# Up projection of a gated MLP: from TensorE transposes to 32x32 transposes on VectorE and regrouping transfers within SBUF

## The chip, the cores and the metric

The kernel runs on one core of a Trainium2 chip. The metric is the device time of one execution in microseconds, the median of three runs. The work of the core is spread over TensorE (PE), VectorE (DVE), ScalarE (ACT), GpSimd (POOL) and the queue of SyncE (SP), which issues nearly all DMA transfers.

## What is computed

One decoder layer on 256 tokens of width 2048, in float32: a parallel mixer (two kinds of attention), a cross attention into 256 memory tokens, and a gated MLP with a causal convolution of width 3 along the tokens, then a last RMSNorm. The change is in the MLP alone:

```python
def conv_ffn(h, w_up, conv_w, conv_b, w_down):
    u = causal_depthwise_conv(h @ w_up, conv_w, conv_b)
    gate, val = u[..., :D_FF], u[..., D_FF:]
    return (jax.nn.silu(gate) * val) @ w_down
```

`D_FF` is 5632, so `w_up` has 2 x 5632 columns. The convolution mixes each feature's own values of three neighbouring tokens, with three weights and a bias per feature.

## The kernel before, in words

**Products.** Every projection is cut into units of 512 output columns (`product`, line 177). A unit keeps two PSUM tiles, one for each block of 128 tokens, and runs over the rows of the weight in blocks of 128. The weights come in transfers of four such blocks (1 MB, `raw`, three buffers, issued on SP at line 190). Each transfer is split in two halves of two row blocks. For precision each half is split into a high and a low part (`split_w`): ACT casts the high part (line 162), DVE subtracts to get the low part (line 163), into two pools of three buffers. Then twelve matmuls run on a half: two row blocks, two token blocks, three products of parts (lines 168 to 170). A unit of the up projection has 16 row blocks, so four transfers, eight halves and 96 matmuls.

**Work between the products.** `tick` is called once per half, while the program is written. Work that is left for later is a generator in `tasks`; `spawn(gen, d)` puts it in the program d halves later, and each `yield n` leaves n halves more. A scheduler then orders the instructions of PE, ACT, DVE and POOL. The queue of SP is kept in the order in which the program is written.

**The MLP (lines 553 to 589).** There are 22 up units. Unit i holds 256 gate columns and the 256 value columns that go with them. When its matmuls are done, ACT copies both PSUM tiles into SBUF, scaled by the norm of each token (`zu`, line 588). Two halves later `gated` turns the unit feature-major: eight PE transposes of 128 x 128 (line 562) into PSUM tiles `uT`, so that features lie on partitions and tokens run along the free dimension. The convolution then takes, for each of four blocks of 128 features, one ACT instruction (line 568) and two DVE instructions (lines 570 and 572) on 256 tokens. Sigmoid, two products and a split into two parts (`gT`, lines 576 to 580) make the left operand of the down projection (`dn`), which follows with 44 row blocks per unit.

```python
    for i in range(KF // 2):
        ps = product(x2T, w_up, i, KD, f"up{i}")
        z = [wk.tile([P, U], F32, tag="w2", name=f"zu{t}") for t in range(NT)]
        for t in range(NT):
            nc.scalar.activation(out=z[t], in_=ps[t], func=AF.Copy, scale=r2[:, t:t + 1])
        spawn(gated(i, z), 2)
```

**Pools.** `b4` has 34 buffers of 4 KB per partition: in the MLP the eight tiles of `x2T`, the four of the residual `xr`, and the `gT` tiles as they are made, 22 at the end.

Of the kernel before, what the change touches and what calls it, by code (L numbers as in the profile page):

```python
# [16 lines left out]
P = 128  # L17
S = 256          # tokens
NT = S // P      # token blocks
D = 2048  # L20
KD = D // P      # 128-row blocks of the model width
FF = 5632
KF = FF // P
U = 512          # columns of one product unit
KB = 4           # 128-row blocks per weight transfer
# [6 lines left out]
# columns of the packed per-partition parameters  # L32
# [13 lines left out]
def hybrid_layer(ctx: ExitStack, tc: tile.TileContext, x, xT, mem, memT, gmix, par, gfin,  # L46
# [28 lines left out]
    # additive masks of the diagonal blocks: [q, k] -> 0 where k <= q (k < q), else NEG  # L75
# [8 lines left out]
    # Work that is emitted between the products: generators that yield the number of  # L84
    # half blocks of weights to let pass before they go on.
# [27 lines left out]
    def split(dst, src, gains=None):  # L113
        """dst[:, 0] + dst[:, 1] = src, or src * gain, in two parts of 12 bits.
        dst [P, 2, 2, S], src [P, 2, S]; gains: a [P, 1] column per 128-row block."""
# [10 lines left out]

    def transposed(dst, src, n, name, gains=None):
        """dst: act tiles of the 4 row blocks n*4.. of the transpose; src [P, NT, U]."""
# [16 lines left out]
    def rstd(ss, n, width, name):  # L145
        """(sum over the last axis of ss [P, n, m] / width + EPS) ** -0.5 -> [P, n]"""
# [19 lines left out]
    def mm3(out, a, b, start=True, stop=True):  # L166
        """out (+)= (a[0] + a[1]).T @ (b[0] + b[1]) without the product of the two low parts."""
        nc.tensor.matmul(out, lhsT=a[0], rhs=b[0], start=start, stop=False)  # L168
        nc.tensor.matmul(out, lhsT=a[0], rhs=b[1], start=False, stop=False)  # L169
        nc.tensor.matmul(out, lhsT=a[1], rhs=b[0], start=False, stop=stop)  # L170
# [6 lines left out]
    def product(xs, w, u, kt_n, name, pieces=None, before=None, heap=False):  # L177
        """x @ w[:, unit u] for both token blocks -> two PSUM tiles [P, U].
        pieces: 128-row blocks per transfer; before(kt): called ahead of the transfer from kt on."""
# [25 lines left out]
    def load_split(src, gains, i, name):  # L205
        """Split act tile i of a transposed input [P, KD, S] in DRAM, scaled by gains."""
# [27 lines left out]
    def proj_T2(ps, r, name):  # L234
        """Evacuate a unit scaled by r and transpose it: act tiles of heads 0, 1 and 2, 3."""
# [7 lines left out]
    def proj_T(ps, r, name, rotate=False):  # L243
        """Evacuate a unit scaled by r and transpose it: [P (dim), 4 (head), S]."""
# [21 lines left out]
    def proj_n(ps, r, name):  # L266
        """Evacuate a unit scaled by r: [P (token), NT, U]."""
# [5 lines left out]
    def attn_T(a, name):  # L273
        """Causal weights of one head [q block][P, K] -> [P (key), 3 * P]:
        keys 0 for both query blocks, then keys 1 for query block 1."""
# [8 lines left out]
    # differential attention  # L284
    oaT = [None] * 4

    def diff_head(h):
        qT, kT, v, hh = qa[h // 4], ka[h // 4], va[h // 4], h % 4
        # scores of the two maps, in a bank each: query block 0 in 0:P, query block 1 in P:3 * P
# [62 lines left out]
    # stick-breaking attention, two heads at a time  # L352
    obT = [None] * 4

    def stick_pair(g):
        aw = [[], []]
        for i in range(NT):
# [14 lines left out]
            # softplus(z) = max(z, 0) + ln(1 + exp(-|z|)), zero where masked  # L372
# [27 lines left out]
    # the input projection in units; the attention of a group of heads runs between the products  # L400
# [21 lines left out]
    # lam = exp(q1.k1) - exp(q2.k2) + LAM_INIT, negated, on all partitions  # L422
# [33 lines left out]
    # branch projections, gated and merged  # L456
# [18 lines left out]
    # output projection and residual  # L475
# [77 lines left out]
    gT = [None] * (KF // 2)  # L553

    def gated(i, z):
        us = []
        for part in range(2):          # gate, value
# [154 lines left out]
```

## Time and profile before

| | |
|---|---|
| time, median of 3 runs (lowest to highest) | 1521.37 us (1520.65 to 1521.76) |
| span of the profiled execution | 1518.9 us; the median of the runs lies 2.5 us above it, which is taken as the time around the span |
| busy, share of the span | PE 99%, DVE 59%, ACT 52%, POOL 4% |
| granted TensorE clock | full (2.4 GHz) in all 40 slices |
| DMA | 287.78 MB, 189 GB/s over the span |
| up projection, from about 753 to 1250 us | 22 units |

The profile is one execution. "Busy" counts the time in which an engine has an instruction at work. Each view below is one question put to the trace of that execution; times in a timeline count from the start of the span.

### The profile page before, as it was taken

The page shows a single profiled execution, that of the slowest core. Times are in us where ns is not written, and L with a number is a line of the kernel's source. Part 1 is how long each engine was busy: PE and PEld are TensorE (multiplying, and loading weights), DVE is VectorE, ACT ScalarE, POOL GpSimd, SP SyncE. Part 2 cuts the span into 40 slices and gives each one's busy share as a digit, 9 for nine tenths or more (in the row PEclk, how much of TensorE's full clock was granted, in tenths as well). Part 3 has the DMA queues.
Part 4 walks back from the last instruction along what each step waited for, and adds up shares of the span by engine and source line. Part 5 has one row for each costly group of instructions (what it writes and reads, how often), then busy time and mean ns, then how long its engine had stood idle before and what let it go on. Part 6 is the DMA issues. An engine that isn't in the chain of part 4 may idle for free.

```text
span 1518.9 us, 17599 instructions
## 1 busy us (share of the span) xinstructions
PE 1503.4 (99%) x6904; PEld 1243.2 (82%) x6904; DVE 896.7 (59%) x1131; ACT 784.7 (52%) x1074; POOL 53.7 (4%) x72
## 2 busy tenths in 40 slices
PE   8999999999999999999999999999999999999997
PEld 6878788888888888888888888888888888888886
DVE  5575666564444565664666667666666666444562
ACT  6454555465555344664565555555555555344441
POOL 0202000000000010000000000000000000000010
PEclk9999999999999999999999999999999999999999
DMA  9544444445555556755355555555555555655561
GB/s 349 187 159 152 162 166 167 167 166 194 194 194 193 183 193 246 265 197 192 139 191 174 189 194 178 183 194 185 179 191 192 174 190 192 222 194 192 197 230 73
DMA packets 44003, 287.78 MB, mean 189 GB/s; under 512 B 5008, under 2 KB 5008, under 8 KB 11152
## 3 DMA queue, kind: packets, MB, share of 16 engines
q1 hardware_dynamic: 43488, 286.13, 54.5%
q8 instruction: 54, 0.88, 0.2%
q10 hardware_dynamic: 432, 0.53, 0.1%
q14 instruction: 29, 0.24, 0.0%
HBM read 284.54 MB, written 2.10 MB: 189 GB/s over the span
## 4 chain that ended last, share of the span: by engine, by line
PE 98%; issue 1%; DMA 0%; DVE 0%; ACT 0%; SPq 0%; POOLq 0%; POOL 0%; DVEq 0%
PE up_mm L170 11%; PE up_mm L169 11%; PE up_mm L168 11%; PE dn_mm L168 5%; PE dn_mm L170 5%; PE dn_mm L169 5%; PE g_mm L168 4%; PE g_mm L169 4%; PE g_mm L170 4%; PE wo_mm L170 2%; PE wo_mm L168 2%; PE wo_mm L169 2%; PE uT L562 1%; PE va_mm L169 1%; PE qb_mm L169 1%; PE qb_mm L168 1%
## 5 line engine op out<-in xcount | busy, mean ns | idle before, releaser
L163 DVE TENSOR_TENSOR up_lo<-up_raw,up_hi 128x1024 fp32r<-128x1024 f32 x176 | 215.7, 1226 | 170.3 <-ACT up_hi L162 167.8
L162 ACT CAST up_hi<-up_raw 128x1024 fp32r<-128x1024 f32 x176 | 185.5, 1054 | 197.5 <-PE up_mm L170 176.5
L170 PE MATMUL up_mm<-up_hi,x2T 128*128 128x512 f32 x704 | 274.1, 389 | 0.0
L169 PE MATMUL up_mm<-up_lo,x2T 128*128 128x512 f32 x704 | 274.0, 389 | 0.0
L168 PE MATMUL up_mm<-up_hi,x2T 128*128 128x512 f32 x704 | 254.8, 392 | 0.0
L163 DVE TENSOR_TENSOR dn_lo<-dn_raw,dn_hi 128x1024 fp32r<-128x1024 f32 x88 | 109.9, 1253 | 101.0 <-ACT dn_hi L162 95.7
L170 PEld LDWEIGHTS up_mm<-up_hi,x2T 128*128 128x128 f32 x704 | 132.2, 188 | 27.4
L169 PEld LDWEIGHTS up_mm<-up_lo,x2T 128*128 128x128 f32 x704 | 132.3, 188 | 26.7
L168 PEld LDWEIGHTS up_mm<-up_hi,x2T 128*128 128x128 f32 x704 | 132.2, 188 | 26.6
L162 ACT CAST dn_hi<-dn_raw 128x1024 fp32r<-128x1024 f32 x88 | 92.0, 1056 | 118.0 <-PE dn_mm L170 103.7
L170 PE MATMUL dn_mm<-dn_hi,gT 128*128 128x512 f32 x352 | 136.9, 389 | 0.0
L169 PE MATMUL dn_mm<-dn_lo,gT 128*128 128x512 f32 x352 | 136.9, 389 | 0.0
L163 DVE TENSOR_TENSOR g_lo<-g_raw,g_hi 128x1024 fp32r<-128x1024 f32 x64 | 78.4, 1225 | 83.8 <-ACT g_hi L162 83.8
L168 PE MATMUL dn_mm<-dn_hi,gT 128*128 128x512 f32 x352 | 126.3, 389 | 0.0
L162 ACT CAST g_hi<-g_raw 128x1024 fp32r<-128x1024 f32 x64 | 67.3, 1053 | 73.4 <-PE g_mm L170 70.2
L169 PE MATMUL g_mm<-g_lo,hT 128*128 128x512 f32 x256 | 100.0, 391 | 0.0
L170 PE MATMUL g_mm<-g_hi,hT 128*128 128x512 f32 x256 | 99.8, 390 | 0.0
L168 PE MATMUL g_mm<-g_hi,hT 128*128 128x512 f32 x256 | 90.7, 391 | 0.0
L170 PEld LDWEIGHTS dn_mm<-dn_hi,gT 128*128 128x128 f32 x352 | 66.1, 188 | 13.8
L169 PEld LDWEIGHTS dn_mm<-dn_lo,gT 128*128 128x128 f32 x352 | 66.1, 188 | 13.7
L168 PEld LDWEIGHTS dn_mm<-dn_hi,gT 128*128 128x128 f32 x352 | 66.1, 188 | 13.6
L170 PEld LDWEIGHTS g_mm<-g_hi,hT 128*128 128x128 f32 x256 | 48.1, 188 | 10.0
(301 smaller groups left out, 2664.5 us busy)
## 6 DMA issues: line engine op xcount, KB each, us to landing
up_raw<-in_w_up SPq DMA_DIRECT2D x88, 1024.0 KB, 4.9
dn_raw<-in_w_dn SPq DMA_DIRECT2D x44, 1024.0 KB, 4.9
g_raw<-in_w_in SPq DMA_DIRECT2D x32, 1024.0 KB, 5.0
wo_raw<-in_w_out SPq DMA_DIRECT2D x16, 1024.0 KB, 5.0
ka_raw<-in_w_in SPq DMA_DIRECT2D x8, 1024.0 KB, 6.1
va_raw<-in_w_in SPq DMA_DIRECT2D x8, 1024.0 KB, 5.0
qb_raw<-in_w_in SPq DMA_DIRECT2D x8, 1024.0 KB, 4.9
kb_raw<-in_w_in SPq DMA_DIRECT2D x8, 1024.0 KB, 4.9
```

Of the source, the lines that this page charges most:

```text
L162: nc.scalar.copy(out=hi, in_=src)
L163: nc.vector.tensor_tensor(out=lo, in0=src, in1=hi.bitcast(F32), op=ALU.subtract)
L168: nc.tensor.matmul(out, lhsT=a[0], rhs=b[0], start=start, stop=False)
L169: nc.tensor.matmul(out, lhsT=a[0], rhs=b[1], start=False, stop=False)
L170: nc.tensor.matmul(out, lhsT=a[1], rhs=b[0], start=False, stop=stop)
L562: nc.tensor.transpose(out=pt[:, j, t * P:(t + 1) * P], in_=z[t][:, c:c + P], identity=ident)
```

## The change

The transposes by PE are taken out. ACT scales the PSUM tile in place (line 603 of the changed kernel). DVE then turns it with one `transpose` instruction per token block (line 129): every 32 x 32 square is turned for itself, so a feature lands on the right one of 32 partitions, but in the wrong group of 32. `regroup` (lines 131 to 139) puts the groups in their places by 16 DMA transfers within SBUF, on the SP queue; each moves 32 partitions x 8 runs of 32 floats, that is 256 runs of 128 bytes. The convolution then reads `uT` in SBUF. `gated` is started five halves after its unit, writes the regrouping, and three halves later the convolution. `blk` and `uT` are two more `b4` tiles. Comments were taken out as well, so the line numbers differ.

```diff
+    def turn(blk, src, t):
+        nc.vector.transpose(out=blk[:, :, t * P:(t + 1) * P], in_=src.rearrange("p (f c) -> p f c", c=P))
+
+    def regroup(dst, blk):
+        q = P // 4
+        d, s = (v.rearrange("p f (t c) -> p (f t) c", t=NT) for v in (dst, blk))
+        for a in range(4):
+            for b in range(4):
+                nc.sync.dma_start(out=d[b * q:(b + 1) * q, :, a * q:(a + 1) * q],
+                                  in_=s[a * q:(a + 1) * q, :, b * q:(b + 1) * q])
+
+    def flip_tile(name):
+        return chunk_tile(f"{name}_blk", [P, U // P, S])
...
-    def gated(i, z):
+    def gated(i, blk):
+        uT = chunk_tile("uT", [P, U // P, S])
+        regroup(uT, blk)
+        yield 3
         us = []
-        for part in range(2):          # gate, value
-            pt = sm_tile("uT").rearrange("p (j s) -> p j s", j=2)
-            for j in range(2):
-                for t in range(NT):
-                    c = (2 * part + j) * P
-                    nc.tensor.transpose(out=pt[:, j, t * P:(t + 1) * P], in_=z[t][:, c:c + P],
-                                        identity=ident)
+        for part in range(2):
             u = wk.tile([P, 2, S], F32, tag="w2", name="u")
             for j in range(2):
                 f = part * KF + 2 * i + j
+                z = uT[:, 2 * part + j]
                 tap = lambda k: col("cw", k * 2 * KF + f)
-                nc.scalar.activation(out=u[:, j], in_=pt[:, j], func=AF.Identity, scale=tap(2),
+                nc.scalar.activation(out=u[:, j], in_=z, func=AF.Identity, scale=tap(2),
                                      bias=col("cb", f))
...
     for i in range(KF // 2):
         ps = product(x2T, w_up, i, KD, f"up{i}")
-        z = [wk.tile([P, U], F32, tag="w2", name=f"zu{t}") for t in range(NT)]
+        blk = flip_tile(f"up{i}")
         for t in range(NT):
-            nc.scalar.activation(out=z[t], in_=ps[t], func=AF.Copy, scale=r2[:, t:t + 1])
-        spawn(gated(i, z), 2)
+            nc.scalar.activation(out=ps[t], in_=ps[t], func=AF.Copy, scale=r2[:, t:t + 1])
+            turn(blk, ps[t], t)
+        spawn(gated(i, blk), 5)
```

Three places in the order of the instructions matter. The first is the queue of SP around the first up units; `up_raw` are the weight transfers, `uT<-up_blk` the regrouping. Before:

```order
L190 DMA qx_raw<-in_w_xq 128x2048 x4
L190 DMA vx_raw<-in_w_xkv 128x2048 x4
L190 DMA wxo_raw<-in_w_xo 128x2048 x4
L190 DMA up_raw<-in_w_up 128x2048 x88
L190 DMA dn_raw<-in_w_dn 128x2048 x11
```

Of the change:

```order
L207 DMA wxo_raw<-in_w_xo 128x2048 x4
L207 DMA up_raw<-in_w_up 128x2048 x7
L138 DMA uT<-up_blk 32x8x32 x16
L207 DMA up_raw<-in_w_up 128x2048 x4
L138 DMA uT<-up_blk 32x8x32 x16
```

The 88 weight transfers stood in one row. Now the 16 regrouping transfers of a unit stand behind the third weight transfer of the next unit (four of unit 0 and three of unit 1 make the seven) and ahead of its fourth, and so on through all 22 units, the last of them among the first transfers of the down projection.

The second place is the end of the regrouping of unit 1 on the same queue, with the waits (DMAHW is one of eight DMA semaphores that are taken in turn):

```order
L138 DMA uT_6478<-up1_blk_6385 32x8x32 [waits DMAHW2_49]
L138 DMA uT_6478<-up1_blk_6385 32x8x32 [waits DMAHW3_49]
L138 DMA uT_6478<-up1_blk_6385 32x8x32 [waits DMAHW4_49]
L138 DMA uT_6478<-up1_blk_6385 32x8x32 [waits DMAHW5_49]
L207 DMA up2_raw_6511<-in_w_up 128x2048 [waits DMAHW6_49,Activation_49]
L207 DMA up3_raw_6573<-in_w_up 128x2048 [waits DMAHW7_49,DVE_49]
```

Each transfer waits until the one eight places ahead of it has landed; the fourth weight transfer of unit 2 (`up2_raw_6511`) is issued only behind the last regrouping transfer of unit 1.

The third place is DVE in one unit, between the end of one unit's matmuls and the low parts of the next. Before:

```order
L163 TENSOR_TENSOR up_lo<-up_raw,up_hi 128x1024 x5
L570 SCALAR_TENSOR_TENSOR u<-uT,pc,u 128x255 x2
L572 SCALAR_TENSOR_TENSOR u<-uT,pc,u 128x254 x2
L163 TENSOR_TENSOR up_lo<-up_raw,up_hi 128x1024
L570 SCALAR_TENSOR_TENSOR u<-uT,pc,u 128x255 x2
L572 SCALAR_TENSOR_TENSOR u<-uT,pc,u 128x254 x2
L163 TENSOR_TENSOR up_lo<-up_raw,up_hi 128x1024
L577 TENSOR_TENSOR u<-u 128x512
```

Of the change:

```order
L129 STREAM_TRANSPOSE up_blk<-up_mm_6209 128x4x128
L129 STREAM_TRANSPOSE up_blk<-up_mm_6210 128x4x128
L180 TENSOR_TENSOR up_lo<-up_raw,up_hi 128x1024 x4
L585 SCALAR_TENSOR_TENSOR u<-uT,pc,u 128x255 x2
L587 SCALAR_TENSOR_TENSOR u<-uT,pc,u 128x254
L585 SCALAR_TENSOR_TENSOR u<-uT,pc,u 128x255
L587 SCALAR_TENSOR_TENSOR u<-uT,pc,u 128x254
L585 SCALAR_TENSOR_TENSOR u<-uT,pc,u 128x255
L587 SCALAR_TENSOR_TENSOR u<-uT,pc,u 128x254 x2
L592 TENSOR_TENSOR u<-u 128x512
L180 TENSOR_TENSOR up_lo<-up_raw,up_hi 128x1024
```

Two low parts of the next unit are made ahead of the transposes. Behind them come four low parts (halves 2 to 5, counted from 0), then the whole convolution of the last unit in one piece and a product, and only then the low part of half 6. On ACT it is the same: four casts, the four instructions of the convolution and the sigmoid, then the cast of half 6. Before, the convolution stood in two pieces with a low part between them.

## Rows read from the trace of the kernel before

**Rows 1.** The page: span, busy time, and the chain that ended last.

```profile
span 1518.9 us, 17599 instructions
PE 1503.4 (99%) x6904; PEld 1243.2 (82%) x6904; DVE 896.7 (59%) x1131; ACT 784.7 (52%) x1074; POOL 53.7 (4%) x72
PE 98%; issue 1%; DMA 0%; DVE 0%; ACT 0%; SPq 0%; POOLq 0%; POOL 0%; DVEq 0%
```

**Rows 2.** Timeline of PE at one unit's transposes: start, duration, instruction.

```profile
980.16 0.39 PE L170 MATMUL up_mm<-up_hi,x2T 128*128 128x512 f32 x1
980.39 1.03 PE L562 MATMUL uT<-ident,zu 128*128 128x128 f32 x8
981.18 0.48 PE L168 MATMUL up_mm<-up_hi,x2T 128*128 128x512 f32 x1
981.50 0.40 PE L169 MATMUL up_mm<-up_lo,x2T 128*128 128x512 f32 x1
```

**Rows 3.** Timeline of PE at the start of up unit 9 (from 0).

```profile
974.95 0.61 PE L168 MATMUL up_mm<-up_hi,x2T 128*128 128x512 f32 x2
975.40 0.39 PE L169 MATMUL up_mm<-up_lo,x2T 128*128 128x512 f32 x1
```

**Rows 4.** Waits of SP's queue from 800 to 1270 us: total, times, longest.

```profile
SPq L190 <- DVE up_lo L163: 431.4, 82, 5.9
```

**Rows 5.** Groups by line, 800 to 1270 us: count, busy us, mean ns, idle before.

```profile
L163 DVE TENSOR_TENSOR up_lo<-up_raw,up_hi 128x1024 fp32r<-128x1024 f32 x164 | 201.0, 1226 | 158.0 <-ACT up_hi L162 155.5
L162 ACT CAST up_hi<-up_raw 128x1024 fp32r<-128x1024 f32 x164 | 172.8, 1054 | 185.2 <-PE up_mm L170 168.5 <-ACT u L568 16.6
L568 ACT ACTIVATE u<-uT,pc 128x256 f32<-128x256 f32 x84 | 42.6, 556 | 0.0
L570 DVE SCALAR_TENSOR_TENSOR u<-uT,pc,u 128x255 f32<-128x255 f32 x84 | 36.5, 476 | 0.0
L577 DVE TENSOR_TENSOR u<-u 128x512 f32<-128x512 f32 x21 | 14.4, 686 | 0.7 <-ACT sg L576 0.7
L576 ACT ACT_TABLE_LOAD x1 | 1.3, 1283 | 0.0
```

**Rows 6.** Groups by line and shape, DVE, whole span: a copy from PSUM.

```profile
L260 DVE COPY kaT<-kaT_tp 128x512 f32<-128x512 f32 x4 | 2.8, 688 | 2.0 <-PE kaT_tp L258 2.0
```

**Rows 7.** Timelines of ACT and DVE in unit 9.

```profile
974.47 1.37 ACT L588 ACTIVATE zu<-up_mm,r 128x512 f32<-128x512 f32 x2 [0.93 <-PE up_mm L170]
980.59 1.05 ACT L162 CAST up_hi<-up_raw 128x1024 fp32r<-128x1024 f32 x1 [1.67 <-PE up_mm L170]
...
982.82 0.87 DVE L570 SCALAR_TENSOR_TENSOR u<-uT,pc,u 128x255 f32<-128x255 f32 x2
```

**Rows 8.** Timeline of SP's queue in unit 9, and DMA issues: KB, us to landing.

```profile
974.82 0.33 SPq L190 DMA_DIRECT2D up_raw<-in_w_up  x1
...
up_raw<-in_w_up SPq DMA_DIRECT2D x88, 1024.0 KB, 4.9
```

**Rows 9.** Timeline of SP's queue at the program's start.

```profile
1.18 0.89 SPq L190 DMA_DIRECT2D qa_raw<-in_w_in  x2
2.12 0.43 SPq L208 DMA_DIRECT2D hT_raw<-in_xT  x1
...
4.98 1.34 SPq L418 DMA_DIRECT2D pc<-in_par  x1
```

**Rows 10.** DMA queues, 0 to 6 us: packets, MB, share of 16 engines.

```profile
q10 hardware_dynamic: 144, 0.01, 1.6%
```

**Rows 11.** Line 621, the stores of the output (256 KB each): landing.

```profile
DMA to landing us min/median/max: 2.0/2.3/2.8
```

**Rows 12.** Sums of one up unit: PE, PEld, DVE, ACT, POOL, clock, DMA share.

```profile
974.95:997.60 22.65, 22.65 (x105) 18.85 (x104) 14.80 (x19) 12.63 (x17) 0.00 (x0) 1.00 0.55 186
```

More of the change, by code (lines that the diff above doesn't have):

```diff
@@ L566, in gated @@
                 f = part * KF + 2 * i + j
+                z = uT[:, 2 * part + j]
                 tap = lambda k: col("cw", k * 2 * KF + f)
-                nc.scalar.activation(out=u[:, j], in_=pt[:, j], func=AF.Identity, scale=tap(2),
+                nc.scalar.activation(out=u[:, j], in_=z, func=AF.Identity, scale=tap(2),
                                      bias=col("cb", f))
-                nc.vector.scalar_tensor_tensor(out=u[:, j, 1:], in0=pt[:, j, 0:S - 1], scalar=tap(1),
+                nc.vector.scalar_tensor_tensor(out=u[:, j, 1:], in0=z[:, 0:S - 1], scalar=tap(1),
                                                in1=u[:, j, 1:], op0=ALU.mult, op1=ALU.add)
-                nc.vector.scalar_tensor_tensor(out=u[:, j, 2:], in0=pt[:, j, 0:S - 2], scalar=tap(0),
+                nc.vector.scalar_tensor_tensor(out=u[:, j, 2:], in0=z[:, 0:S - 2], scalar=tap(0),
                                                in1=u[:, j, 2:], op0=ALU.mult, op1=ALU.add)
```

## The prediction

> **What bounds the kernel now.** I read the page first: PE is busy for 1503.4 of 1518.9 us and makes 98% of the chain that ended last [rows 1]. So only what PE executes, or what makes PE wait, changes the time. The timeline of PE at a unit's transposes then gives their price: the reader should see that matmuls start in an even step, and that this step breaks around the eight transposes [rows 2]. Next come the waits of SP's queue: 431.4 us of these 470 us it waits for DVE to free a weight buffer [rows 4]. The queue has time to spare, but each weight transfer leaves the moment its buffer is free, so whatever stands ahead of it can delay it. The question is how late the fourth weight transfer and the convolution may be before PE starves, so I lay out one unit on a clock.
>
> **The clock of a unit.** Let 0 be the first matmul of a unit, at 974.95. Two matmul starts take 975.40 - 974.95 = 0.45 us [rows 3], so a step is 0.227 us (96 steps and the transposes make the 22.65 us of rows 12), a half of 12 matmuls 2.72 us, and a unit without transposes 21.8 us. Half 6 starts at 6 x 2.72 = 16.32; its first two matmuls use the high part alone, the third the low part [rows 3]: the low part of half 6 is due at 16.77.
>
> **What goes away.** Between the last matmul before the transposes (980.16) and the second one behind them (981.50) lie 1.34 us, where two steps would take 0.45 [rows 2]. So eight transposes cost PE 0.89 us, and 22 units **19.5 us**. PE has no wait there, so all of it comes off the end if nothing new makes PE wait. ACT's copy becomes a scaling in place, of the same size; at nothing. The convolution reads SBUF instead of PSUM; I keep the old durations.
>
> **What is added on DVE.** Two transposes of 128x512 per unit. The trace has no such instruction; the nearest row is a copy of 128x512 from PSUM, 0.69 us [rows 6]. I take that; the lower bound is 0.48 (a 255-element instruction [rows 5]), the upper twice the copy, 1.38. DVE works 14.8 of 22.65 us in a unit [rows 12], so 1.4 us more fit. ACT scales the two PSUM tiles from -0.48 to 0.89 [rows 7], the second transpose ends at 0.89 + 0.03 + 0.69 = 1.61, and SP's queue issues the first regrouping transfer at **1.7**. Until then the queue stands still, since the third weight transfer was issued in the unit before. Behind it wait the fourth weight transfer (which was issued at 974.82, that is at -0.13 [rows 8]) and the first of the next unit.
>
> **What is added on SP's queue.** 16 transfers per unit. Issued one behind the other, transfers take a step of (2.12 - 1.18)/2 = 0.47 us [rows 9]; one alone takes 0.33 [rows 8]. All of these have 128 runs, the new ones 256 shorter runs. I take 0.47, the row of back-to-back issues; the bounds are 0.33 and 0.47 + 0.33 = 0.80 (the whole of a lone issue once more for 128 more runs). The ninth transfer waits until the first has landed: eight steps are 3.8 us, the stores of the output land after 2.0 to 2.8 us [rows 11], so this wait is empty.
>
> **Load path.** The fourth weight transfer is issued at 1.7 + 16 x 0.47 = 9.22 and lands 4.9 us later [rows 8], at 14.12. Cast (1.05) and low part (1.23) [rows 5] with two hand-overs of 0.03 give 16.46. Due at 16.77: **0.3 us to spare**.
>
> **Convolution path.** The last regrouping transfer is issued at 1.7 + 15 x 0.47 = 8.75. I take 2.0 us to landing, the fastest store, because these move an eighth of its bytes: 10.75. First ACT instruction 0.56, hand-over 0.05: 11.36. Eight DVE instructions at a step of 0.87 - 0.48 = 0.39 [rows 7], the last one whole: 7 x 0.39 + 0.48 = 3.2, so 14.56. Product 0.69, with 0.03 between: 15.28. Low part of half 6, 1.23: 16.54. **0.2 us to spare.** Meanwhile ACT does sigmoid and cast, which end by 15.2. The next half's low part follows two instructions later, at 18.5, and is due at 19.5.
>
> So both paths just fit. The break-even step is (16.77 - 2.34 - 4.9 - 1.7)/16 = 0.489 us on the load path and 0.47 + 0.23/15 = 0.485 on the other. Above that each 0.1 us per issue costs PE 1.6 us in each unit, 35 us in all.
>
> **DMA engines.** They are 55% busy in a unit, 12.4 us [rows 12]. The only small packets in the trace are the 64-byte rows of one load at the start: 144 packets in 1.6% of 16 x 6 us, 10.7 ns each [rows 10]. For 128 bytes, at the rate of the big transfers (1 MB in some 3 us over 16 engines), 3 ns more: 14 ns. An engine gets 16 x 16 such packets and 16 semaphore writes per unit: 3.7 us. 12.4 + 3.7 = 16.1 of 21.8 us, so it fits, and per transfer (0.23 us) it is below the issue step.
>
> **Once only.** The table load of 1.28 us before the first sigmoid [rows 5] now lies between convolution and cast; with 0.8 us of slack on ACT it costs about 0.5 us once. The two more tiles per unit fit in the 34 buffers: 8 + 4 + 20 `gT` leave two at the end, whose readers are transfers that landed a unit before.
>
> **Sum.** -19.5 + 0.5 = -19.0 us: a span of 1499.9 against the 1518.9 of the profiled execution, and with the 2.5 us around it 1502.4, the same as 19.0 off the median 1521.37. Forecast **1502 us**, for itself 1500 to 1506 (0.01 us of overrun per issue is 3.5 us).
>
> **Rivals.**
> 1. *The issue step grows with the number of runs* (slower). The mechanism: SP's queue holds the fourth weight transfer behind 16 issues of more than 0.49 us each. For it speaks that an issue takes longer when much is queued: 1.34 us for one transfer of 128 runs behind eight others [rows 9]. Against it, that one waits for bytes to drain, and the new transfers drain in 0.23 us. If half of the 0.33 us is paid again the step is 0.635: (0.635 - 0.489) x 16 = 2.3 us per unit, 51 in all, 1554 us; if all of it, 0.80: 5.0 us, 109 in all, 1612 us.
> 2. *The slack is used up by a smaller delay.* If the regrouping lands after 2.8 us instead of 2.0, the convolution path overruns by 0.57 us, 12.5 in all: 1515. If a transpose takes 1.38 us, everything starts 1.4 us later, less 0.3 of slack: 24 us, 1526.
> 3. *The DMA engines become the bound.* If 128 bytes took as long as 2 KB, which at the big transfers' rate is some 90 ns, an engine would need 256 x 0.09 = 23 us for a unit's regrouping beside 12.4 for weights: 35 us per unit, 290 us slower, about 1800. The 10.7 ns of rows 10 speak against it; those packets ran from HBM, not within SBUF.
>
> A rule of the Trainium skill speaks for the first rival: Perfetto Trace Analysis, sections "DMA Instruction — HWDGE (DVE, Sync)" and "What \"DMA-bound\" means", says that an issue's profiled time is the generation of its descriptors, and that large descriptors are what helps a busy issuing queue. By that rule alone the 256 runs would make the step the 0.80 of the upper bound, and the time 1612 us. The trace agrees only that the issue has a time of its own; no row has another number of runs, so it leaves the rule open.
>
> **How the numbers follow.** Forecast 0.42. Rival 1 0.33, because the price of 256 runs is the one term with no row and the slack is only 4% of a step. Rival 2 0.17. Rival 3 0.08. A measurement here can tell about 0.2%, 3 us, from no change. Faster: the forecast and 0.10 of rival 2, 0.52. Same: 0.04 of rival 2 and 0.01 of rival 1, 0.05. Slower: the rest of rival 1 (0.32), rival 3 and 0.03 of rival 2, 0.43. The range runs from 1500 to 1585: above it lie rival 3 and 0.10 of rival 1, below it 0.02.
>
> **What would show it.** Right: 16 issues per unit at a step near 0.47 us; PE's starts even through each unit, 21.8 us apart from unit to unit; no wait of PE for `up_hi` or `up_lo`; DMA share near 0.74 there. Wrong: issues of 0.6 us or more; in each unit a gap of PE ahead of half 6, ended by the low part, with the cast waiting for `up_raw` (rival 1) or for the convolution's instructions, which wait for `uT` (rivals 1 and 2); DMA near 1.0 (rival 3). A transpose well above 0.69 us would show the second form of rival 2. If PE's step were even and the time still not 15 us lower, the price of the transposes would be wrong.

## The result and the profile after

The changed kernel takes **1625.46 us** (median of 4 runs, 1623.44 to 1626.31), the kernel before 1521.28 beside it: 1.0684 times as long, 95% interval 1.0671 to 1.0697. It is slower by 104 us, where 19 us less were forecast, and it lies above the range. The profiled execution has a span of 1624.5 us.

The page of the changed kernel, with the lines that answer to [rows 1] (span, busy time, chain), and three groups of its fifth part (line, engine, operation, count, busy us, mean ns, idle before and what ended it):

```profile
span 1624.5 us, 17843 instructions
PE 1531.6 (94%) x6728; PEld 1245.5 (77%) x6728; DVE 928.8 (57%) x1175; ACT 787.2 (48%) x1074; POOL 53.7 (3%) x72
PE 70%; SPq 14%; DMA 7%; DVE 4%; ACT 3%; issue 2%; POOLq 0%; POOL 0%; ACTq 0%; DVEq 0%
...
L185 PE MATMUL up_mm<-up_hi,x2T 128*128 128x512 f32 x704 | 258.3, 410 | 66.7 <-ACT up_hi L179 66.7
L186 PE MATMUL up_mm<-up_lo,x2T 128*128 128x512 f32 x704 | 290.6, 413 | 7.6 <-DVE up_lo L180 7.3
...
L583 ACT ACTIVATE u<-uT,pc 128x256 f32<-128x256 f32 x88 | 45.7, 591 | 112.9 <-DMA uT<-up_blk 112.9
```

PE fell from 98% of the chain to 70%, and the queue of SP stands in it with 14%. PE waits for `up_hi`, the convolution for `uT`; neither wait was there before. The PE work is as forecast: 176 matmul records fewer (the 22 x 8 transposes).

What the queue does in unit 15, whose first matmul starts at 1179.16 (timeline of SP; then the first line of what the trace says of line 138: ns min/median/max; then two DMA groups: KB, us to landing):

```profile
1181.25 10.39 SPq L138 DMA_DIRECT2D uT<-up_blk  x16
1191.73 2.23 SPq L207 DMA_DIRECT2D up_raw<-in_w_up  x3
...
L138 SPq DMA_DIRECT2D uT<-up_blk x352: 585/609/1870, 795.5 to 1383.7; - x176
...
up_raw<-in_w_up SPq DMA_DIRECT2D x88, 1024.0 KB, 5.8
uT<-up_blk SPq DMA_DIRECT2D x352, 32.0 KB, 1.9
```

Sixteen issues run from 2.09 to 12.48 on the unit's clock (PE's first matmul at 0, as in the prediction), a step of (10.39 - 0.61)/15 = **0.65 us**. Behind them the fourth weight transfer is issued at 12.58 and lands 5.8 us later, at 18.39. The last regrouping transfer lands at 14.7. What follows on ACT and PE:

```profile
1196.83 0.63 ACT L591 ACTIVATE sg<-u 128x512 f32<-128x512 f32 x1 [0.81 <-DVE u L587]
1197.63 2.00 ACT L179 CAST up_hi<-up_raw 128x1024 fp32r<-128x1024 f32 x2 [0.17 <-DMA up_raw<-in_w_up]
...
1198.73 0.73 PE L185 MATMUL up_mm<-up_hi,x2T 128*128 128x512 f32 x2 [3.09 <-ACT up_hi L179]
1199.99 0.68 PE L186 MATMUL up_mm<-up_lo,x2T 128*128 128x512 f32 x1 [0.53 <-DVE up_lo L180]
1200.46 0.63 PE L187 MATMUL up_mm<-up_hi,x2T 128*128 128x512 f32 x1
1200.89 0.63 PE L186 MATMUL up_mm<-up_lo,x2T 128*128 128x512 f32 x1
```

ACT is through with the convolution's part at 1197.46 and waits another 0.17 us for the weights: both paths of the prediction end within a fifth of a microsecond of each other, both some 4 us after the time at which the cast of half 6 had to start (14.4). In the other units they end within 0.75 us of each other, and in 20 of 21 units the weights come last. Half 6 starts at 19.57 on the unit's clock instead of 16.32. Then PE's step is 0.43 us instead of the 0.227 of [rows 3]. The windows of the same stretch (length, busy of PE, PEld, DVE, ACT, POOL, granted clock, DMA share, GB/s) show why:

```profile
1179.16:1195.40 16.24, 16.24 (x73) 13.33 (x71) 7.12 (x8) 6.89 (x9) 0.00 (x0) 1.00 0.31 63
1195.40:1198.70 3.30, 0.24 (x2) 0.00 (x0) 3.20 (x8) 2.32 (x5) 0.00 (x0) 1.00 1.01 425
1198.70:1201.00 2.30, 1.75 (x5) 1.13 (x6) 2.30 (x4) 1.82 (x2) 0.00 (x0) 0.81 1.00 424
1201.00:1204.00 3.00, 3.00 (x10) 2.33 (x9) 2.41 (x3) 0.67 (x2) 0.00 (x0) 0.57 0.68 213
```

After PE has stood for 3 us, the granted clock falls to its lower level, 1.2 GHz, for some 3.4 us. That does not happen in every unit, and the length of a unit follows it. Unit 3, with 6.8 us at the lower level, and unit 4, with none (the granted clock is the third figure from the end):

```profile
849.02:878.19 29.17, 25.24 (x97) 19.83 (x96) 16.25 (x21) 12.77 (x17) 0.00 (x0) 0.88 0.50 162
878.19:903.53 25.34, 22.34 (x97) 17.86 (x96) 16.25 (x21) 12.78 (x17) 0.00 (x0) 1.00 0.54 175
```

The three units without a fall (4, 8 and 12) take 25.3 to 25.6 us, the five with 6.8 us take 28.4 to 29.3. Over all, a unit takes 25.3 to 29.3 us, 27.5 in the mean, instead of 22.65.

### The profile page after: what moved, and what is told of

Read it like the earlier page. It is cut to its first block, busy times and chain, and to the rows that moved or that the text cites. A ratio compares the mean times of both kernels' runs of the same rounds, so it can differ in the third digit from the quotient of the medians.

```text
span 1624.5 us, 17843 instructions
## 1 busy us (share of the span) xinstructions
PE 1531.6 (94%) x6728; PEld 1245.5 (77%) x6728; DVE 928.8 (57%) x1175; ACT 787.2 (48%) x1074; POOL 53.7 (3%) x72
## 4 chain that ended last, share of the span: by engine, by line
PE 70%; SPq 14%; DMA 7%; DVE 4%; ACT 3%; issue 2%; POOLq 0%; POOL 0%; ACTq 0%; DVEq 0%
SPq L138 14%; DMA up_raw<-in_w_up 7%; PE dn_mm L185 4%; PE dn_mm L186 4%; PE dn_mm L187 4%; PE up_mm L186 4%; PE g_mm L186 4%; PE g_mm L185 4%; PE g_mm L187 4%; PE up_mm L185 3%; PE up_mm L187 3%; DVE up_blk L129 2%; PE wo_mm L185 2%; PE wo_mm L186 2%; PE wo_mm L187 2%
## 5 line engine op out<-in xcount | busy, mean ns | idle before, releaser
L185 PE MATMUL up_mm<-up_hi,x2T 128*128 128x512 f32 x704 | 258.3, 410 | 66.7 <-ACT up_hi L179 66.7
L186 PE MATMUL up_mm<-up_lo,x2T 128*128 128x512 f32 x704 | 290.6, 413 | 7.6 <-DVE up_lo L180 7.3
L187 PE MATMUL up_mm<-up_hi,x2T 128*128 128x512 f32 x704 | 286.7, 407 | 0.0
L185 PEld LDWEIGHTS up_mm<-up_hi,x2T 128*128 128x128 f32 x704 | 138.1, 199 | 104.3 <-ACT up_hi L179 75.5
L186 PEld LDWEIGHTS up_mm<-up_lo,x2T 128*128 128x128 f32 x704 | 140.4, 199 | 48.6 <-DVE up_lo L180 19.0
L187 PEld LDWEIGHTS up_mm<-up_hi,x2T 128*128 128x128 f32 x704 | 140.2, 199 | 29.3
L583 ACT ACTIVATE u<-uT,pc 128x256 f32<-128x256 f32 x88 | 45.7, 591 | 112.9 <-DMA uT<-up_blk 112.9
L585 DVE SCALAR_TENSOR_TENSOR u<-uT,pc,u 128x255 f32<-128x255 f32 x88 | 42.3, 481 | 99.4 <-ACT u L583 99.3
L185 PEld LDWEIGHTS dn_mm<-dn_hi,gT 128*128 128x128 f32 x352 | 66.3, 189 | 18.3 <-ACT dn_hi L179 4.6
```

Source lines behind the costliest of these rows:

```text
L583: nc.scalar.activation(out=u[:, j], in_=z, func=AF.Identity, scale=tap(2), bias=col("cb", f))
L585: nc.vector.scalar_tensor_tensor(out=u[:, j, 1:], in0=z[:, 0:S - 1], scalar=tap(1), in1=u[:, j, 1:], op0=ALU.mult, op1=ALU.add)
```

## The experiments

Three questions: what sets the 0.65 us; which of the two late paths holds PE; and whether the sum of the prediction is there once nothing is late. Line numbers in the rows shift by a few from kernel to kernel. The first four runs follow from the profile above alone.

**Regrouping behind the fourth weight transfer.** `spawn(gated(i, blk), 5)` becomes `..., 7)`, and `yield 3` behind `regroup` becomes `yield 1`.

> One edit: the 16 regrouping transfers are written two halves later, so that they stand behind the fourth weight transfer of a unit instead of ahead of it; all instructions are the same. The scheduler then also puts the convolution behind half 7 instead of ahead of half 6. Theory A (the queue of SP holds the fourth weight transfer behind 16 issues of 0.65 us, and ACT and DVE stand at the convolution for the last of them): both waits are gone, PE runs even, 1502 to 1508 us, and the issues still take 0.65 us each. Theory B (the cost is in the DMA engines, which carry 90112 packets of 128 bytes more, or in the transposes on DVE): nothing of that is removed, 1600 to 1626 us.

Measured: 1511.96 us, 0.9937 times the time before (0.9923 to 0.995). The step is still 0.65 us. The main loss is gone, though some 10 us over the forecast remain. One cause shows in the trace: the next unit's first weight transfer now stands behind the sixteen issues. The first low part of unit 15 ends at 1.19 on its clock, due at 0.45; the cast of unit 16 waits for its weights:

```profile
1126.88 1.05 ACT L179 CAST up_hi<-up_raw 128x1024 fp32r<-128x1024 f32 x1 [1.79 <-DMA up_raw<-in_w_up]
```

**Convolution later.** `yield 3` becomes `yield 8`.

> One edit: the convolution is written eight halves behind its regrouping instead of three, so that it never waits for it; the queue of SP is in the same order as in the changed kernel. Theory A1 (the fourth weight transfer is late by itself): it is still issued at about 12.6 us of the unit and lands at 18.4, PE waits as before, 1605 to 1627 us. Theory A2 (only the convolution that waits for the regrouping holds up ACT and DVE; the weights would come in time): 1502 to 1510 us.

Measured: 1628.69 us, 1.0712 (1.0697 to 1.0727). This tells nothing: the scheduler put the convolution back to where it was, behind the fourth of the casts, and the convolution waits as before (waits, total, times, longest):

```profile
ACT u L583 <- DMA uT<-up_blk: 112.6, 22, 6.3
```

**Half the runs per transfer.** 128 runs of 256 bytes instead of 256 of 128; the pieces land in wrong places.

```diff
-                nc.sync.dma_start(out=d[b * q:(b + 1) * q, :, a * q:(a + 1) * q],
-                                  in_=s[a * q:(a + 1) * q, :, b * q:(b + 1) * q])
+                nc.sync.dma_start(out=dst[b * q:(b + 1) * q, :, a * 64:(a + 1) * 64],
+                                  in_=blk[a * q:(a + 1) * q, :, b * 64:(b + 1) * 64])
```

> The 16 transfers keep their number, their 32 partitions and their bytes, but move 4 runs of 64 floats per partition instead of 8 runs of 32: 128 runs of 256 bytes each. The pieces go to wrong places, so the output isn't the layer's. If the price of an issue is set by its runs (0.33 us for 128 alone, 0.61 for 256: 2.2 ns a run), the step falls to 0.38 to 0.47 us, the fourth weight transfer is issued at 8.5 to 9.7 us instead of 12.6, and the time is 1502 to 1520 us. If it is set by the transfer within SBUF or by its 32 partitions, whatever the runs, the step stays at 0.65 and the time at 1615 to 1630 us.

Measured: 1595.92 us, 1.0498 (1.048 to 1.0516). The issue time hardly moved (0.599 us for 0.609):

```profile
L135 SPq DMA_DIRECT2D uT<-up_blk x352: 585/599/1818, 795.0 to 1360.3; - x176
```

So the number of runs does not set it, and the expectation fell. The 30 us go with an earlier start: the first transfers now read one token block alone, so they wait for the first transpose only and begin at 1.41 instead of 2.09, and the clock is lower for less of the time (0.982 of full speed in the mean, 0.973 in the change).

**Matmuls in the wait.** Ahead of half 6's wait PE gets 14 matmuls more in every unit but the first, with half 5's operands, into a PSUM tile that nobody reads.

> The changed kernel with 14 more matmuls in each up unit but the first, around half 5, that read half 5's high part and write a PSUM tile that nobody reads: 3.2 us of work where PE otherwise waits 3 to 4 us for half 6. If the fall of the granted clock to its lower level behind each wait costs time of its own (3.4 us at half speed per unit, 1.7 us lost), it no longer falls or falls less often, and with 294 matmuls more the kernel is faster than the changed one: 1585 to 1600 us. If the lower clock costs nothing because half 7 is late anyway, the time stays at 1620 to 1630 us; if the added matmuls push back half 6, it is above.

Measured: 1593.83 us, 1.0484 (1.047 to 1.0498), clock 0.998 instead of 0.973. As expected: 32 us go with the fallen clock. The waits alone are worth 1593.8 - 1500 = 94 us; the 1500 is the time without a wait, which the next runs measure. Together they are the 125 us by which the change lies above 1500.

The next four ask for the price and for the path.

**Eight transfers of 64 partitions.**

```diff
-        for a in range(4):
+        for a in range(2):
             for b in range(4):
-                nc.sync.dma_start(out=d[b * q:(b + 1) * q, :, a * q:(a + 1) * q],
-                                  in_=s[a * q:(a + 1) * q, :, b * q:(b + 1) * q])
+                nc.sync.dma_start(out=d[a * 64:(a + 1) * 64, :, b * q:(b + 1) * q],
+                                  in_=s[(1 - a) * 64:(2 - a) * 64, :, b * q:(b + 1) * q])
```

> Eight transfers of 64 partitions with eight runs of 128 bytes each take the place of the sixteen of 32 partitions; the bytes of a unit are the same, the pieces land in wrong places. Theory A (the issue has a price per transfer, whatever its runs and partitions): each issue takes 0.55 to 0.70 us, the regroup is issued within 5.2 us instead of 10.4, load 3 and the convolution come in time, 1500 to 1520 us. Theory B (the price follows the partitions of a transfer): an issue takes about 1.2 us, the regroup is as long as before, 1595 to 1630 us.

Measured: **1500.28 us** (2 runs), 0.9865 (0.9845 to 0.9884); every unit from the second on takes 21.76 us. 64 partitions and 512 runs cost as much as 32 and 256:

```profile
L136 SPq DMA_DIRECT2D uT<-up_blk x176: 596/634/1533, 795.7 to 1258.1; - x176
```

**One run per partition.** 32 runs of 1024 bytes: `out=dst[b * q:(b + 1) * q, a, :]`, `in_=blk[a * q:(a + 1) * q, b, :]`.

> Sixteen transfers as in the change, but each moves one unbroken run of 1024 bytes for each of 32 partitions, so a transfer has 32 runs instead of 256; the blocks land in wrong places. Theory A (the price belongs to a transfer within SBUF as such): issue 0.55 to 0.65 us, time 1590 to 1630 us. Theory B (the price belongs to a pattern of two dimensions on each partition, which no transfer of the kernel before has): issue 0.33 to 0.48 us, time 1500 to 1530 us.

Measured: 1588.81 us, 1.0447 (1.0426 to 1.0468). Theory A:

```profile
L135 SPq DMA_DIRECT2D uT<-up_blk x352: 507/588/1888, 795.9 to 1347.3; - x176
```

**The same from DRAM.** As the last one, but `in_=x[a, b * q:(b + 1) * q, 0, 0:S]`, the layer's input.

> Sixteen transfers of 32 partitions with one run of 1024 bytes each stand in the regroup's place in the queue, but read columns of the input x in DRAM instead of the transposed tile (the convolution then works on the input's numbers). Only the issue time is asked. Theory A (a source within SBUF makes the issue 0.6 us): 0.30 to 0.40 us each, like the weight transfers. Rival (32 partitions, or sixteen issues in a row, make it 0.6 us): 0.55 to 0.65 us. The time of the kernel: 1500 to 1510 us under either, since these transfers wait for nothing and are issued ahead of the unit's start.

Measured: 1500.28 us, one run. Issues take 0.42 us at a step of 0.46, a little above what was expected:

```profile
L135 SPq DMA_DIRECT2D uT<-in_x x352: 310/419/802, 788.9 to 1254.3; - x176
```

The transfers of these two runs differ in the source alone (those from DRAM also go out sooner, as they wait for nothing). Within SBUF an issue of the same 32 runs is 0.17 us longer. It is not the source alone that does it: the stores of the output, from SBUF to DRAM, are cheap to issue in the kernel before:

```profile
L621 SPq DMA_DIRECT2D out<-xr x6: 333/385/448, 1504.6 to 1513.7; - x6
```

Those stores stand by themselves, but so does the first of each sixteen transfers of the change, and it takes 0.59 us (median) like the others. So the dearer issue goes with both ends in SBUF, and the 0.47 of [rows 9], all from DRAM, was a right price for the wrong kind of transfer.

**Convolution without the wait.** The regrouping stays where the change has it, but the convolution reads `x2T[2 * (2 * part + j)][:, 0, 0]` and no longer waits for it.

> The regroup is issued as in the change, ahead of the fourth weight transfer, but the convolution reads columns of x2T in place of the regrouped tile, so nothing on ScalarE or VectorE waits for the regroup; uT is written and not read. Theory A (the weight transfer queued behind the sixteen issues is enough to set the time; the convolution's wait only rides along): 1590 to 1625 us, with ScalarE's cast of half 6 still waiting for the weight transfer in nearly every unit. Theory B (the convolution's wait on the two engines sets it): 1500 to 1515 us, and no wait of the matmuls for half 6.

Measured: 1616.93 us, 1.063 (1.0615 to 1.0646): theory A. ACT stands idle and waits for the weights alone (waits of the whole span, and unit 15):

```profile
ACT up_hi L179 <- DMA up_raw<-in_w_up: 181.9, 39, 10.1
...
1193.72 1.99 ACT L179 CAST up_hi<-up_raw 128x1024 fp32r<-128x1024 f32 x2 [8.36 <-DMA up_raw<-in_w_up]
```

The load path is enough for 117 of the 125 us that separate the change from 1500.

**Four groups of four**, each behind one of the next four weight transfers: `regroup(uT, blk, a)` for one `a` at a time, `yield 2` between them, `spawn(..., 7)`.

> The sixteen transfers are issued in four groups of four, one behind each of the next four weight transfers, and the convolution follows the last; all of the change's work is done. Theory A (what costs is a weight transfer that stands behind more issues than its slack covers; four issues are 2.6 us): no weight transfer is late, 1500 to 1506 us, which is the sum of the prediction without a wait. Rival (the 10 us that were left in the run with the regroup behind the fourth weight transfer come from the regroup's packets slowing the weight transfers, or from the longer evacuation): 1508 to 1514 us.

Measured: 1558.92 us, 1.024 (1.0218 to 1.0261); both missed. The weight transfers are in time, but the scheduler turned the order of ACT around: the evacuations (line 603), which wait for the unit's last matmul, now stand ahead of the next unit's first cast, so PE stops between the units:

```profile
1131.64 1.34 ACT L603 ACTIVATE up_mm<-up_mm,r 128x512 f32<-128x512 f32 x2 [5.91 <-PE up_mm L186]
1132.91 2.93 ACT L178 CAST up_hi<-up_raw 128x1024 fp32r<-128x1024 f32 x3
...
1133.99 0.73 PE L184 MATMUL up_mm<-up_hi,x2T 128*128 128x512 f32 x2 [1.71 <-ACT up_hi L178]
```

Then other queues, and other places on the same queue.

**Two queues, SP and POOL.** `(nc.sync, nc.gpsimd)[b % 2].dma_start(...)`.

> Of the sixteen transfers of a regroup eight are issued on SyncE's queue as before and eight on GpSimd's, which stands idle in this part; all of the change's work is done. The scheduler now puts the convolution behind the first cast of the next unit. Theory A (16 issues of 0.65 us on one queue are what delays the weight transfer and the convolution): SyncE's eight end 5.2 us after the first, at about 7.3, so the fourth weight transfer comes in time, and GpSimd's eight are in time if one takes under 1.7 us there: 1499 to 1506 us. Rival (the price belongs to the transfer's way through SBUF and the DMA engines, not to the queue, so two queues share it and each issue takes twice as long): 1560 to 1625 us.

Measured: 1617.13 us, 1.0638 (1.0621 to 1.0655). Neither theory: the scheduler put the transposes behind two low parts and two products of the unit before on DVE, so in unit 15 (from 1174.00) SP's group began 5 us later, at 7.1, and POOL's at 7.6; in most other units SP's began at 6.5 to 9.3. The fourth weight transfer of unit 15 went out at 12.4 as in the change, and the time is within 0.6% of the change's:

```profile
1179.15 0.69 DVE L593 TENSOR_TENSOR sg<-u,sg 128x512 f32<-128x512 f32 x1
1179.75 1.31 DVE L129 STREAM_TRANSPOSE up_blk<-up_mm 128x512 f32<-128x512 f32 x2
...
1181.09 5.18 SPq L138 DMA_DIRECT2D uT<-up_blk  x8
1186.37 1.19 SPq L207 DMA_DIRECT2D up_raw<-in_w_up  x1
```

**All on POOL.** `nc.gpsimd.dma_start(...)` for all sixteen.

> All sixteen transfers of a regroup are issued on GpSimd's queue; SyncE's queue then holds the weight transfers alone, as before the change. Theory A: no weight transfer waits, and the convolution, which the scheduler puts behind the first cast of the next unit, is in time if an issue takes less than about 0.87 us there: 1499 to 1506 us; with a dearer issue every unit would be as long as the sixteen, so 1.5 us each would give about 24 us a unit, 1550 us. Rival (the regroup's packets on the DMA engines hold the weight transfers back, whichever queue issues them): 1515 us or more, with the casts waiting for weight transfers.

Measured: 1643.98 us, 1.0809 (1.0793 to 1.0826). Inconclusive on the time: in the scheduler's order a unit's transposes stand behind the convolution of the unit before, and the first matmul two units on starts as they end, which fits a wait for the PSUM tile that they read (the trace names an ACT cast that ends at the same time). What can be read is the price of an issue, the same on this queue:

```profile
L138 POOL DMA_DIRECT2D uT<-up_blk x352: 584/584/775, 796.4 to 1426.5; - x176
```

**SP and ACT.** `(nc.sync, nc.scalar)[b % 2].dma_start(...)`.

> Of the sixteen transfers eight are issued on SyncE's queue and eight on ScalarE's, between its casts; all of the change's work is done, and the two transposes stay right behind the evacuations. Theory A (the price belongs to the queue that issues: two queues issue at the same time, each 0.6 us a transfer): the fourth weight transfer is issued at about 7.5 as in the run with eight transfers, ScalarE's eight issues, 4.8 us, fit into its idle time before the casts are due: 1499 to 1507 us. Rival (two queues share one price, so that each issue takes about 1.2 us while both issue): the fourth weight transfer again at 12, 1590 to 1625 us.

Measured: 1641.83 us, 1.0794 (1.0779 to 1.0809). The price is theory A's: both queues issue at the same time, each at its 0.6 us (only ACT's third issue takes 0.86 in the median), and the fourth weight transfer goes out at 6.9 (unit 15, from 1199.72). The time is not. ACT's last issues come behind that weight transfer, the last of them lands 7.4 us after its issue (11.4 in the worst unit), and the convolution waits on ACT ahead of the casts of halves 6 and 7:

```profile
L138 ACTq DMA_DIRECT2D uT<-up_blk x176: 592/622/885, 795.8 to 1407.6; - x176
L138 SPq DMA_DIRECT2D uT<-up_blk x176: 585/609/1807, 795.8 to 1406.8; - x176
...
1206.66 4.92 SPq L207 DMA_DIRECT2D up_raw<-in_w_up  x3
...
1215.63 2.08 ACT L583 ACTIVATE u<-uT,pc 128x256 f32<-128x256 f32 x4 [5.66 <-DMA uT<-up_blk]
1217.61 1.98 ACT L179 CAST up_hi<-up_raw 128x1024 fp32r<-128x1024 f32 x2
```

This is the convolution path by itself: the weights of half 6 had landed at 12.5, and its cast began at 17.9. Either path can hold PE alone; the regrouped tile, though, landed about 1 us later here (15.8) than in the change (14.7).

**Two groups of eight**, behind the fourth weight transfer and behind the next unit's first: `regroup(uT, blk, h)` with `a` in `range(2 * h, 2 * h + 2)`, `yield 2` between, `spawn(..., 7)`.

> The sixteen transfers stay on SyncE's queue in two groups of eight, one behind the fourth weight transfer and one behind the next unit's first; all of the change's work is done, and the scheduler keeps the next unit's first two casts ahead of the evacuations, unlike in the run with four groups. Theory A: eight issues are 5.2 us, which fit between two weight transfers, so none is late and the 10 us left in the run with the regroup behind the fourth weight transfer go: 1499 to 1506 us. Rival (what was left there has another cause than the next unit's first weight transfer behind the sixteen issues): 1509 to 1515 us as there.

Measured: 1508.89 us, 0.9922 (0.9905 to 0.9938). At the edge of the rival's range: nine of 21 units take 21.8 us or less, the others up to 23.1, and ACT waits 59.9 us in all for the regrouped tile, ahead of the next unit's first casts. Of the 12 us that the first run had left above 1500 only 3 went, so the next unit's first weight transfer was not the main part of them. What holds these units the next run shows more plainly.

**Half ahead, half behind** the fourth weight transfer: as the last one with `spawn(..., 5)`.

> The sixteen transfers stay on SyncE's queue in two groups of eight, one ahead of the fourth weight transfer as in the change and one behind it; all of the change's work is done. Theory A (issue step 0.65 us, one queue, nothing else): the first group ends at about 7.3, as in the run with eight transfers, so the fourth weight transfer comes in time; the second ends at about 13, lands at 15, and the next unit's first weight transfer goes out then, some 4 us late and still landing before the unit's first cast, which waits about 0.1 to 0.3 us a unit for the convolution: 1500 to 1508 us. Rival (what the runs with the regroup behind the fourth transfer had left, 9 to 12 us above 1500, comes with any regroup of sixteen transfers, whatever its place): 1509 to 1515 us.

Measured: 1526.64 us, 1.0036 (1.0024 to 1.0049); both missed. The units settle at about 22.8 us. Here ACT shows a chain that goes once around per unit: the late convolution holds the next unit's casts, these hold the evacuations, and those the transposes, so that the next regrouping starts at 4.0 instead of 2.1 and its convolution is late again:

```profile
1130.10 2.00 ACT L179 CAST up_hi<-up_raw 128x1024 fp32r<-128x1024 f32 x2 [5.04 <-DMA up_raw<-in_w_up]
1132.65 2.08 ACT L585 ACTIVATE u<-uT,pc 128x256 f32<-128x256 f32 x4 [0.54 <-DMA uT<-up_blk]
1135.61 0.63 ACT L593 ACTIVATE sg<-u 128x512 f32<-128x512 f32 x1 [0.88 <-DVE u L589]
1136.47 2.00 ACT L179 CAST up_hi<-up_raw 128x1024 fp32r<-128x1024 f32 x2 [0.22 <-DMA up_raw<-in_w_up]
1138.37 1.23 ACT L605 ACTIVATE up_mm<-up_mm,r 128x512 f32<-128x512 f32 x2
```

**The convolution a unit later.** Moving the code does not move the convolution (second run), so its bias goes through a tile that also reads the next unit's sums, times zero:

```diff
+        bt = st.tile([P, 4], F32, tag="bt", name="bt")
+        nc.vector.scalar_tensor_tensor(out=bt[:, 2 * part:2 * part + 2], in0=last[i + 1][:, 0:2],
+                                       scalar=0.0, in1=c, op0=ALU.mult, op1=ALU.add)
...
-                                     bias=col("cb", f))
+                                     bias=bt[:, 2 * part + j:2 * part + j + 1])
```

> The regroup in two groups of eight on SyncE's queue, behind the fourth weight transfer and behind the next unit's first, and the convolution a unit later: its bias passes through a small tile that also reads the next unit's sums, so that it can't stand ahead of that unit's evacuations; all of the work is done, with two small VectorE operations a unit more. Theory A (what the full-work runs had left above 1500 us is a chain that runs once around per unit: transposes, regroup, convolution, and behind the convolution on ScalarE and VectorE the next unit's first casts, evacuations and transposes): the chain is cut, the regroup starts at about 3.5 again, no weight transfer stands behind more than eight issues, 1499 to 1506 us, with at most some 0.2 us a unit for a low part behind the convolution. Rival (the sixteen issues or their packets cost by themselves, wherever they stand): 1508 us or more, as in the runs before.

Measured: 1515.05 us, 0.9961 (0.9947 to 0.9974). The chain is cut, the regrouping starts at 1.6 and no weight transfer is late, but DVE now works on the convolution when half 2's low part is due. In unit 15 (from 1107.58) it ends at 6.4, due at 5.9, and each unit takes 22.5 us:

```profile
1112.37 0.48 DVE L598 SCALAR_TENSOR_TENSOR u<-uT,pc,u 128x254 f32<-128x254 f32 x1
1112.77 1.22 DVE L180 TENSOR_TENSOR up_lo<-up_raw,up_hi 128x1024 fp32r<-128x1024 f32 x1
```

**The convolution behind half 3.** The tile reads the low part of half 3 instead, and the two groups go behind the next unit's first and second weight transfers (`spawn(..., 9)`).

> As the run before, with two things moved: the two groups of eight stand behind the next unit's first and second weight transfers, and the convolution's bias passes through a small tile that reads the low part of half 3, so the convolution stands behind the casts and low parts of halves 2 and 3, a unit after its products. All of the work is done. Theory A (in the run before only the low part of half 2 was late, behind the convolution on VectorE, 0.73 us a unit; sixteen issues cost nothing where no weight transfer, cast, low part or evacuation due sooner stands behind them): the units run at their 21.76 us, 1499.5 to 1504 us. Rival (the sixteen issues or their packets cost by themselves): 1508 us or more.

Measured: **1500.43 us** (1500.41 to 1500.89), 0.9865 (0.9849 to 0.9882) of the time before, with all of the work done. It beats both kernels. Unit 15 as in [rows 12]; the issues are as dear as ever, and the regrouping takes up to 7.2 us to land, but nothing that is due sooner stands behind either:

```profile
1098.84:1120.60 21.76, 21.76 (x98) 18.02 (x96) 16.39 (x23) 12.71 (x17) 0.00 (x0) 1.00 0.69 211
...
L138 SPq DMA_DIRECT2D uT<-up_blk x352: 585/608/2184, 799.8 to 1268.7; - x176
DMA to landing us min/median/max: 1.9/3.7/7.2
```

## Why the prediction was wrong

The forecast failed at one step: "I take 0.47, the row of back-to-back issues". The step is 0.65, inside the bounds given and above the break-even of 0.485. The mechanism behind that step, sixteen issues on SP's queue ahead of the fourth weight transfer, was seen rightly, in rival 1.

- **What goes away, 0.89 us a unit:** right. 22.65 - 21.76 = 0.89, and the runs without a wait stand at 1500.3 and 1500.4 us against the 1502.4 of the sum. Of the whole gain of 21 us, 2.1 lie behind the up units (249.5 us from the last unit's end in the kernel before, which is at 1269 us and not at about 1250, and 247.4 in the last run): 0.9 of them are the last unit's transposes, what made the rest is open.
- **Transposes, 0.69 us each:** right; two follow each other in 1.31 to 1.4 us. The start of the regrouping was put at 1.7; it was 2.09, as ACT's scaling began at -0.03 instead of -0.48.
- **Issue step:** mis-sized by 0.65 - 0.47 = 0.18 us, sixteen times, 2.9 us a unit. The rows it was taken from are transfers from DRAM; no row of the kernel before has both ends in SBUF.
- **Load path, 0.3 us to spare:** with the measured terms of unit 15 it is 2.09 + 16 x 0.65 + 0.1 + 5.8 + 2.34 = 20.73, due at 16.77: 4.0 us late. Of these 2.9 are the step, 0.9 the landing (5.8 for 4.9; two more weight transfers go out within the same 2.2 us, at a DMA share of 1.01), 0.4 the start, 0.1 the step to the next issue, less 0.3 of slack. Unit 15 has the longest landing: in the mean of 21 units it is 5.35, and since in some units one of the issues takes up to 1.87 us, the weight transfer is issued at 13.1, which makes 20.9. Times 22 the 4.0 us are 87 us; the run with matmuls in the wait, where the clock held, has 94.
- **Convolution path, 0.2 us to spare:** late as well. In the mean of 21 units ACT is through with it at 18.1, where the cast of half 6 had to start at 14.4; the weights let it start at 18.5. So with the weights in time PE would still have waited, by this trace some 0.4 us less in each unit.
- **The clock:** no step of the prediction had it. Behind 18 of the 21 waits (2.8 to 4.3 us each) 3.4 to 6.8 us at the lower level followed. With one more behind the up units that is 82 us at half speed, at most 41 us lost; by the run with matmuls in the wait it is 32. The load path's 87 and these 32 on top of 1500 make 1619 of the measured 1625; some 6 us are left open.
- **DMA engines (rival 3):** out. A packet of 128 bytes took 12 ns (14 forecast), and the same bytes in the same packets run in 1500.4 us.

Rival 1 named the mechanism and its place; its price for half of a second issue, 0.635, came near the 0.65, and its 1554 was short by the landing, the start and the clock. Its stated cause fell: the price hardly grows with the number of runs. 32, 128, 256 and 512 runs took 0.59, 0.60, 0.61 and 0.63 us. The rule of the Trainium skill that was weighed beside it (Perfetto Trace Analysis, "DMA Instruction — HWDGE (DVE, Sync)" and "What "DMA-bound" means") led to 0.80 us and 1612 us. The runs disagree with the rule, since fewer and larger pieces shortened an issue by 0.02 us at most (256 runs of 128 bytes to 32 of 1024). The measured time came close to 1612 by another road. What both ends in SBUF add to an issue is measured; why they do is open. Of rival 2's causes the transpose of 1.38 us did not appear (0.7). The landing of 2.8 us did in part: the last transfer of a regrouping landed after 1.9 us in most units, but after 2.8 to 3.2 in five of 22, unit 15 among them. That is the convolution path, which was late by more than this anyway.

The range failed too: its upper end of 1585 left out the dearer part of rival 1, and no term stood for a wait that costs more than its length or for a weight transfer that lands later than before.

## What to carry to other kernels

Before a queue gets many small transfers, take the price of an issue from a transfer of the same kind, with the same memory at both ends, multiply it by their number, and ask which transfer with a due time stands behind them. Small pieces that need not be ready soon belong where nothing due stands behind them, and their reader a whole unit later: with the same sixteen transfers the kernel is 104 us slower than before in one place and 21 us faster in another. Where a scheduler sets the order, look at the order of every engine after each edit: a moved piece of code may not move at all, and something else may move instead.

## What the runs showed of the hardware

- The issue of a transfer within SBUF took 0.58 to 0.63 us (medians) on the queues of SP, ACT and POOL alike; with a source in DRAM and the same 32 runs of 1024 bytes it took 0.42, and stores from SBUF to DRAM took 0.33 to 0.45. With SP and POOL, or SP and ACT, issuing at the same time SP's step stayed at 0.65 us.
- Packets of 128 bytes within SBUF took 12 to 13 ns on the queues of SP and ACT; 90112 of them were no bound.
- In the change the granted clock fell to 1.2 GHz behind 18 of 21 waits of PE of 2.8 to 4.3 us, for 3.4 to 6.8 us. Where PE had other matmuls in that time it stayed up through all up units.
- A small transfer issued right behind a 1 MB weight transfer landed 3.5 to 5.3 us after its issue (medians of three runs, up to 7.2) instead of 1.9. On ACT's queue, behind a weight transfer of SP's, the last one took 7.4 (median).
